# Two projections moved to the other pool of PSUM banks, a gate projection in two passes, and the last statistics drawn together

## The chip, the cores and the metric

The kernel runs on one core of one Trainium2 chip. The metric is the device time of one execution in microseconds. Three runs of the kernel before gave 1345.57, 1344.99 and 1338.48 us (median 1344.99). The profiled execution took 1340.82 us, of which 1338.9 us are the span from its first to its last instruction.

## The reference

The program is a two-layer decoder trunk on 512 positions of 1024 channels, in float32. Each layer normalises, makes one wide projection, runs four token mixers on slices of it, projects back, and adds a gated feed-forward block:

```python
for l in range(DEPTH):                      # DEPTH = 2
    h = rms_norm(x, norm_mix_w[l])
    proj = h @ w_in[l]                      # 1024 -> 3592 columns
    rq, rk, rv, rg, ca, cg, gq, gk, gv, gg, gb, ga, hq, hf, hi, hgate = split(proj)
    ret  = head_group_norm(retention(rq, rk, rv)) * silu(rg)
    conf = conformer_conv(ca, cg, ...)
    gq, gk, gv = split(silu(causal_depthwise_conv(concat(gq, gk, gv))))     # 4 taps
    gdn  = head_rms_norm(gated_deltanet(gq, gk, gv, beta=gb, a=ga)) * silu(gg)
    hg   = head_rms_norm(hgrn2(hq, hf, hi)) * silu(hgate)
    x = x + concat(ret, conf, gdn, hg) @ w_out[l]
    h = rms_norm(x, norm_ffn_w[l])
    x = x + (silu(h @ gate[l]) * (h @ up[l])) @ down[l]                     # 2816 hidden
return rms_norm(x, final_norm_w)
```

What matters here is the start of each layer: the projections `gk`, `gq` of the delta rule, each followed by a causal convolution of 4 taps and a SiLU, and its gate projection `gg` (256 gate columns with `gb` and `ga`, 264 in all). At the very end it is the last `rms_norm`.

## The kernel before, in words

Activations lie with channels on the 128 partitions and the 512 positions along the row, as eight tiles `x0` to `x7`. Every float32 product is made from three fast ones: an operand is split into a rounded high part and the rest (`xh`/`xl`, `whi`/`wlo`), and high*high, low*high and high*low are summed in one PSUM bank (`mm3`, L455 to L457). Weights come by DMA on the SP queue; ScalarE rounds them (L257), GpSimd takes the rest (L258).

PSUM has eight banks, in two pools of four. `pd` serves the projections, `pm` the mixers and the statistics. A pool hands its banks out in turn, and a matmul into a bank waits until whatever used it last is finished.

`layer` walks through `ORDER`: gk0, gk1, gq0, gq1, gg, gv0, and so on. A projection of 128 channels (`dense_c`) takes one bank: 8 blocks of input, 3 matmuls each. In layer 0 the first two go together (`dense_c2`). `gg` has positions on the partitions (`dense_t`, L493 to L495): four blocks of positions, one `pd` bank each, 96 matmuls of 264 columns.

The norm is applied after the projection. `rstd_sum` (L231) sums the squares over the channels on TensorE, VectorE scales (L235), GpSimd takes the power (L213) and writes `rst`; `rstd_spread` (L242) turns it into a row on all partitions, and ScalarE copies it into `rsb` (L246). `R_SUM` says after which projection the sum is issued; the spread follows one projection later.

What frees a bank of gk or gq is `conv4`: VectorE multiplies by `rsb` in place (L596), ScalarE makes the first tap (L598), VectorE the other three (L600), ScalarE a tanh back into the bank (L602), and VectorE the last product (L603). The two tiles `y` are shared: gk0 and gq0 use one, gk1 and gq1 the other. What frees a bank of `gg` is a tanh on ScalarE (L613), a product on VectorE (L614), and two small ones (L650, L651).

The order on each engine is not that of the code: a scheduler arranges the instructions engine by engine when the kernel is built, by its own estimate of times. On the chip each engine then goes strictly through its list.

At the end of layer 1 the last two of eight output tiles are made in two halves of 256 positions. The first half's squares are summed when all its tiles are there. `leave(half)` spreads the result, copies it to `rsb`, multiplies the eight tiles (five on VectorE from the bank, L1671, three on GpSimd from `rsb`, L1669) and issues eight DMAs of 128 KB (L1672), four each on the ScalarE and the SP queue.

Of the kernel before, what the change touches and what calls it, by code (L numbers as in the profile page):

```python
# [7 lines left out]
F32 = mybir.dt.float32  # L8
# [8 lines left out]
P = 128  # L17
T = 512
NB = T // P
D = 1024  # L20
KD = D // P
H = 4
HD = 64
G = 256
D_FF = 2816
KF = D_FF // P
DEPTH = 2
# [2 lines left out]
WARM = 4  # L30
EU, ET = 0, 0
N_OUT = 4
R_SUM = [1, 0]
TAIL = 2
CONF_POOL = 7
CHUNK_K = 2
# [30 lines left out]
           gg=2304, hq=2568, hf=2824, hi=3080, hgate=3336)  # L67
# [71 lines left out]
def kernel(  # L139
# [15 lines left out]
    V, S, GP, PE = nc.vector, nc.scalar, nc.gpsimd, nc.tensor  # L155
# [37 lines left out]
    def sm(n, name, dt=F32):  # L193
        return small.tile([P, n], dt, name=name)
# [219 lines left out]
    def w_next(keep=0):  # L414

        i = pos[2]
        pos[2] += 1
        for q in held.values():
            q[:] = [n for n in q if n >= i - keep]
        p = piece_of(items[i])  # L420
        w_split(i + 1)
        assert i in halves
        w_load(p + 3)
        w_split(i + 2)
        while pos[1] < min(i + 1 + AHEAD, len(items)) and len(items[pos[1]]) == 2 and extra:
# [17 lines left out]
    def tick():  # L443
        for it in list(active):
            if it[3] > 0:
                it[3] -= 1
            elif resume(it[0], it[1] + (it[2],)) == "end":
                active.remove(it)
            else:
                it[2] += 1  # L450
                it[3] = lag_of(it[1], it[2])
# [4 lines left out]
        PE.matmul(ps, hi[:, w], al, start=False, stop=False, skip_group_check=shared)  # L456
        PE.matmul(ps, lo[:, w], ah, start=False, stop=last, skip_group_check=shared)  # L457

    def dense_c(ah, al, ks):

        hv = w_next()
        ps = pd.tile([P, T], F32, name="pd")
        for n in range(KD):
            mm3(ps, *hv[n // 4], n % 4, ah[ks[n]], al[ks[n]], n == 0, n == KD - 1)
            if n % CHUNK_K == CHUNK_K - 1:
                tick()
        return ps

    def dense_c2():

        hv = [w_next(q) for q in range(2)]
        ps = [pd.tile([P, T], F32, name="pd") for _ in range(2)]
        for k in range(KD):
            for q in range(2):
                mm3(ps[q], *hv[q][k // 4], k % 4, xh[k], xl[k], k == 0, k == KD - 1)
            tick()
        return ps

    def dense_t(n):

        per = 1 if n > 256 else 2
        ps = [pd.tile([P, T], F32, name="pd") for _ in range(NB // per)]
        for g in range(2):
            hv = w_next()
            for hf in range(2):
                hi, lo = hv[hf]
                for kk in range(2):
                    k = g * 4 + hf * 2 + kk
                    w = slice(kk * n, (kk + 1) * n)
                    for b in range(NB):  # L490
                        o = ps[b // per][:, (b % per) * n:(b % per) * n + n]
                        tk = slice(b * P, (b + 1) * P)
                        PE.matmul(o, xh[k][:, tk], hi[:, w], start=(k == 0 and b % per == 0), stop=False)  # L493
                        PE.matmul(o, xh[k][:, tk], lo[:, w], start=False, stop=False)  # L494
                        PE.matmul(o, xl[k][:, tk], hi[:, w], start=False,  # L495
                                  stop=(k == KD - 1 and b % per == per - 1))
                    if kk % CHUNK_K == CHUNK_K - 1:
                        tick()
        return [ps[b // per][:, (b % per) * n:(b % per) * n + n] for b in range(NB)]
# [87 lines left out]
    def layer(l, ar, ga, open_mix, gvp, gzp):  # L587
# [17 lines left out]
            if len(st["conv"]) == 6:  # L605
                ga.put(*st["cy2"])

        def gate_t(ps4, n=256):

            g = ar.get(4)  # L610
            gv = g.rearrange("p (b c) -> p b c", b=NB)
            for b in range(NB):
                S.activation(gv[:, b, :], ps4[b][:, :G], AF.Tanh, scale=rsh[:, b:b + 1])  # L613
                V.scalar_tensor_tensor(gv[:, b, :], gv[:, b, :], 1.0, ps4[b][:, :G], op0=ADD, op1=MUL)  # L614
            return g

        def val_t(ps4):
            v = ar.get(4)
            vv = v.rearrange("p (b c) -> p b c", b=NB)
            for b in range(NB):  # L620
                S.activation(vv[:, b, :], ps4[b], AF.Copy, scale=rst[:, b:b + 1])
            return v

# [18 lines left out]
            return f  # L642

        def ev_gg(ps4):
            st["gg"] = gate_t(ps4)
            bt = sm(NB * H, "bt")
            z = sm(NB * H, "z")
            st["bt"], st["z"] = bt, z
            for b in range(NB):
                S.activation(bt[:, b * H:(b + 1) * H], ps4[b][:, G:G + H], AF.Tanh, scale=rsh[:, b:b + 1])  # L650
                V.scalar_tensor_tensor(z[:, b * H:(b + 1) * H], ps4[b][:, G + H:G + 2 * H], rst[:, b:b + 1],  # L651
                                       vc[:, o + V_DT:o + V_DT + H], op0=MUL, op1=ADD)
# [63 lines left out]
        for ct in range(2):  # L716
# [1 line left out]
            ev[f"hf{ct}"], ev[f"hq{ct}"] = ev_hf(ct), ev_hq(ct)  # L718
            ev[f"ca{ct}"], ev[f"cg{ct}"] = ev_ca(ct), ev_cg(ct)
            ev[f"rk{ct}"], ev[f"rq{ct}"] = ev_rot("rk", ct), ev_rot("rq", ct)  # L720
        ev["gg"] = ev_gg
        for nm in ("hi", "rv"):
            ev[nm] = (lambda nm: lambda ps4: st.__setitem__(nm, val_t(ps4)))(nm)
        for nm in ("hgate", "rg"):
# [704 lines left out]
        pend = []  # L1429
        for n, nm in enumerate(ORDER):  # L1430
            if nm == "gg":
                ps = dense_t(G + 2 * H)
            elif nm in T_GROUPS:
                ps = dense_t(G)
            elif l == 0 and n < 2:
                if n == 0:
                    first = dense_c2()
                ps = first[n]
            else:
                ps = dense_c(xh, xl, range(KD))  # L1440
            pend.append((nm, ps))
            if n == R_SUM[l]:
                rstd_sum(range(NB), ssq)
            if n < R_SUM[l] + 1:
                continue
            if n == R_SUM[l] + 1:
                rstd_spread()
            for nm, ps in pend:
                while not ar.can(*NEED.get(nm[:2], ())):
                    tick()  # L1450
                ev[nm](ps)
                if nm in after:
# [12 lines left out]
    for l in range(DEPTH):  # L1465
# [47 lines left out]
        with tc.tile_pool(name=f"ffp{l}", bufs=1, reuse_waits="tile") as ffp, \  # L1513
# [149 lines left out]
            def leave(half):  # L1663

                c = slice(half * T // 2, (half + 1) * T // 2)
                pb = rstd_spread(range(2 * half, 2 * half + 2), False)
                for k in range(KD):
                    if k % 3 == 1:
                        GP.tensor_tensor(x[k][:, c], x[k][:, c], rsb[:, c], op=MUL)  # L1669
                    else:  # L1670
                        V.tensor_tensor(x[k][:, c], x[k][:, c], pb[:, c], op=MUL)  # L1671
                    (nc.sync if k % 2 else nc.scalar).dma_start(out[k * P:(k + 1) * P, c], x[k][:, c])  # L1672

            def down_plain(rows):
                order = plain_order(l, rows)
                js = (head, rest)[rows]
                for n_m, (m, c) in enumerate(order):
                    ps = pd.tile([P, T], F32, name="pd")[:, c]
                    for r in runs(rows, n_m == 0):
                        hv = w_next()  # L1680
                        for n, k in enumerate(r):
                            ph, pl = hid[k]
                            mm3(ps, *hv[n // 4], n % 4, ph[:, c], pl[:, c], k == js[0], k == js[-1])
                        finish()
                    if rows and l + 1 == DEPTH and n_m == KD:
                        rstd_sum(range(NB // 2), ssq)
                    if rows and l + 1 == DEPTH and n_m == KD + 1:
                        leave(0)
                    V.tensor_tensor(x[m][:, c], x[m][:, c], ps, op=ADD)
                    if not rows:  # L1690
                        continue
                    if l + 1 < DEPTH:
                        split_x(m, o + NV + V_NMIX)
                        ssq_add(m)
                        nc.sync.dma_start(xs[m * P:(m + 1) * P, :], x[m])
                    else:
                        end = n_m == len(order) - 1
                        sq = ssq_add(m, end, c)
                        S.activation(x[m][:, c], x[m][:, c], AF.Copy, scale=col(V_FIN + m))
                return sq if rows and l + 1 == DEPTH else None  # L1700
# [99 lines left out]
```

## Time and profile before

| | us |
|---|---|
| three runs | 1345.57, 1344.99, 1338.48 |
| profiled execution | 1340.82 |
| its span | 1338.9 |
| TensorE busy | 1289.4 (96%) |
| VectorE busy | 897.7 (67%) |
| GpSimd busy | 799.3 (60%) |
| ScalarE busy | 707.7 (53%) |

A row of the timeline has the start, the time until the group's end, the engine, the line and operation, the tiles written and read, the size and the count; in brackets stands how long the engine was idle before it, and who ended that. PE is TensorE, DVE VectorE, ACT ScalarE, POOL GpSimd; a name with q is an engine's queue of DMA triggers. A row of a table by windows has the stretch, its length, each engine's busy time and count, then the TensorE clock that was granted (1.00 is full), the share of the DMA engines and GB/s.

### The profile page before, as it was taken

To read this page: it belongs to the slowest core of one execution; us is meant where nothing else is said; L and a number is where in the kernel's file an instruction comes from. 1 tells how busy PE (TensorE), PEld (TensorE's weight loads), DVE (VectorE), ACT (ScalarE), POOL (GpSimd) and SP (SyncE) were. 2 spreads that over 40 slices of the span, in tenths; PEclk is the share of its full clock that TensorE was granted. 3 is DMA by queue.
4 is the path that set the end of the run, shared out by engine and by line. 5 is a ranking of instruction groups with operands and counts; after the bars stand their busy time and mean duration, and the time that the engine had idled before them with its cause. 6 is when DMAs were issued, how large, how long until landed. Compare 5 with 4: busy or idle time off the path is not lost.

```text
span 1338.9 us, 23722 instructions
## 1 busy us (share of the span) xinstructions
PE 1289.4 (96%) x8984; PEld 1178.5 (88%) x8984; DVE 897.7 (67%) x1569; ACT 707.7 (53%) x1454; POOL 799.3 (60%) x669
## 2 busy tenths in 40 slices
PE   8799998899999999999999999989999999999996
PEld 6788888887889999999878889889888999999995
DVE  6743678656696866776466348786559777678645
ACT  5452553534456656665445445445445665566554
POOL 6276773764356676577454767747624666566762
PEclk9899998889999999999999999989999999999998
DMA  7223210134142333333442332102423243333322
GB/s 283 64 63 105 82 32 9 33 102 134 33 126 95 111 114 95 108 110 89 127 165 81 88 95 59 32 1 63 153 77 102 80 121 101 111 97 109 119 80 71
DMA packets 60385, 124.50 MB, mean 93 GB/s; under 512 B 17520, under 2 KB 26992, under 8 KB 60272
## 3 DMA queue, kind: packets, MB, share of 16 engines
q1 hardware_dynamic: 58832, 121.83, 29.8%
q8 instruction: 70, 1.15, 0.3%
q10 hardware_dynamic: 1440, 1.18, 0.3%
q14 instruction: 43, 0.35, 0.1%
HBM read 116.17 MB, written 6.82 MB: 92 GB/s over the span
## 4 chain that ended last, share of the span: by engine, by line
PE 84%; DVE 8%; POOL 3%; ACT 3%; issue 1%; DMA 0%; POOLq 0%; SPq 0%; ACTq 0%; DVEq 0%
PE pm L455 12%; PE pm L456 12%; PE pm L457 12%; PE pd L455 11%; PE pd L456 11%; PE pd L457 10%; PE pd L493 3%; PE pd L494 3%; PE pd L495 3%; PE pm L1167 2%; DVE x L1270 2%; PE pm L906 1%; POOL wlo L258 1%; PE pm L1040 1%; PE pm L1029 1%
## 5 line engine op out<-in xcount | busy, mean ns | idle before, releaser
L258 POOL TENSOR_TENSOR wlo<-wraw,whi 128x512 fp32r<-128x512 f32 (+2 forms) x192 | 260.6, 1366 | 226.0 <-ACT whi L257 197.2
L384 POOL TENSOR_TENSOR wlo<-wraw,whi 128x512 fp32r<-128x512 f32 x208 | 272.4, 1329 | 104.9 <-ACT whi L383 100.1
L455 PE MATMUL pm<-bh,whi 128*128 128x256 f32 x1008 | 282.7, 282 | 3.7 <-ACT pm L1623 2.0
L456 PE MATMUL pm<-bl,whi 128*128 128x256 f32 x1008 | 281.4, 280 | 0.0
L457 PE MATMUL pm<-bh,wlo 128*128 128x256 f32 x1008 | 276.8, 280 | 0.0
L257 ACT CAST whi<-wraw 128x512 fp32r<-128x512 f32 (+2 forms) x212 | 125.2, 598 | 195.8 <-PE pd L456 123.3
L455 PEld LDWEIGHTS pm<-bh,whi 128*128 128x128 f32 x1008 | 189.6, 188 | 6.7 <-DVE pm L1633 2.9
L456 PEld LDWEIGHTS pm<-bl,whi 128*128 128x128 f32 x1008 | 190.0, 188 | 0.5
L457 PEld LDWEIGHTS pm<-bh,wlo 128*128 128x128 f32 x1008 | 187.7, 188 | 0.1
L456 PE MATMUL pd<-xl,whi 128*128 128x512 f32 x416 | 165.5, 400 | 2.4 <-DVE xl L252 2.3
L455 PE MATMUL pd<-xh,whi 128*128 128x512 f32 x416 | 164.9, 399 | 0.7 <-ACT xh L251 0.4
L457 PE MATMUL pd<-xh,wlo 128*128 128x512 f32 x416 | 165.0, 399 | 0.0
L383 ACT CAST whi<-wraw 128x512 fp32r<-128x512 f32 x208 | 126.7, 624 | 50.5 <-PE pm L456 41.5
L384 DVE TENSOR_TENSOR wlo<-pd,whi 128x512 fp32r<-128x512 f32 x156 | 107.5, 689 | 52.1 <-ACT whi L383 49.6
L383 ACT CAST whi<-pd 128x512 fp32r<-128x512 f32 x156 | 92.0, 589 | 64.2 <-PE pm L456 22.7
L378 POOL TENSOR_TENSOR wraw<-wraw 128x512 f32<-128x512 f32 x52 | 68.7, 1322 | 79.0 <-DVE pd L366 66.4
L493 PE MATMUL pd<-whi,xh 128*128 128x256 f32 (+1 forms) x320 | 95.9, 301 | 15.0 <-DVE ar L603 8.5
L456 PEld LDWEIGHTS pd<-xl,whi 128*128 128x128 f32 x416 | 79.0, 190 | 21.4 <-DVE xl L252 4.3
L455 PEld LDWEIGHTS pd<-xh,whi 128*128 128x128 f32 x416 | 79.0, 190 | 19.9 <-ACT xh L251 1.8
L494 PE MATMUL pd<-wlo,xh 128*128 128x256 f32 (+1 forms) x320 | 95.4, 299 | 0.0
L495 PE MATMUL pd<-whi,xl 128*128 128x256 f32 (+1 forms) x320 | 95.1, 298 | 0.0
L457 PEld LDWEIGHTS pd<-xh,wlo 128*128 128x128 f32 x416 | 78.7, 189 | 17.4
(354 smaller groups left out, 3117.7 us busy)
## 6 DMA issues: line engine op xcount, KB each, us to landing
wraw<-in_wf_dram SPq DMA_DIRECT2D x88, 512.0 KB, 3.6
wraw<-in_wc_dram SPq DMA_DIRECT2D x34, 512.0 KB, 3.6
wraw<-in_wd_dram SPq DMA_DIRECT2D x32, 512.0 KB, 3.8
wraw<-in_wt_dram SPq DMA_DIRECT2D x16, 512.0 KB, 3.6
wraw<-in_wo_dram SPq DMA_DIRECT2D x32, 256.0 KB, 2.6
x<-in_xt_dram SPq DMA_DIRECT2D x16, 256.0 KB, 3.6
wraw<-in_wd_dram SPq DMA_DIRECT2D x16, 256.0 KB, 2.7
wraw<-in_wd_dram SPq DMA_DIRECT2D x20, 128.0 KB, 2.1
```

The source lines that it names most:

```text
L257: S.copy(hi[:, :n], r)
L258: eng.tensor_tensor(lo[:, :n], r, hi[:, :n].bitcast(F32), op=SUB)
L378: GP.tensor_tensor(src, c, a, op=SUB)
L383: S.copy(hi, src)
L384: eng.tensor_tensor(lo, src, hi.bitcast(F32), op=SUB)
L455: PE.matmul(ps, hi[:, w], ah, start=first, stop=False, skip_group_check=shared)
L456: PE.matmul(ps, hi[:, w], al, start=False, stop=False, skip_group_check=shared)
L457: PE.matmul(ps, lo[:, w], ah, start=False, stop=last, skip_group_check=shared)
L493: PE.matmul(o, xh[k][:, tk], hi[:, w], start=(k == 0 and b % per == 0), stop=False)
L494: PE.matmul(o, xh[k][:, tk], lo[:, w], start=False, stop=False)
L495: PE.matmul(o, xl[k][:, tk], hi[:, w], start=False, stop=(k == KD - 1 and b % per == per - 1))
L1167: PE.matmul(ps[:, (bb * 2 + ct) * P:(bb * 2 + ct + 1) * P], k[:, ct * T + b * P:ct * T + (b + 1) * P], qx[:, (ct * NB + b) * P:(ct * NB + ...
```

## The change

Four edits. The first two projections of each layer take `pm` banks in place of `pd` banks. In layer 0 the sum of squares is issued one projection earlier (`R_SUM`). `gg` is computed in two passes of two blocks of positions, each with two `pd` banks, and each pass is evacuated by itself; the split weights of both input halves stay until the second pass has used them. And at the end `leave(0)` comes behind the second half's sum of squares.

```diff
-R_SUM = [1, 0]
+R_SUM = [0, 0]
...
+    def w_ahead():
+        for q in held.values():
+            q[:] = [n for n in q if n >= pos[2] - 1]
+        w_split(pos[2] + 1)
...
-    def dense_c(ah, al, ks):
+    def dense_c(ah, al, ks, ps=None):
         hv = w_next()
-        ps = pd.tile([P, T], F32, name="pd")
+        if ps is None:
+            ps = pd.tile([P, T], F32, name="pd")
...
     def dense_c2():
         hv = [w_next(q) for q in range(2)]
-        ps = [pd.tile([P, T], F32, name="pd") for _ in range(2)]
+        ps = [pm.tile([P, T], F32, name="pm") for _ in range(2)]
...
+    def dense_t_wide(n):
+        hv = []
+        for part in range(2):
+            blocks = range(2 * part, 2 * part + 2)
+            ps = {b: (pd.tile([P, T], F32, name="pd")[:, :n], True, True) for b in blocks}
+            for g in range(2):
+                if part == 0:
+                    hv.append(w_next(g))
+                elif g:
+                    w_ahead()
+                t_part(ps, hv[g], n, g, blocks)
+            yield {b: ps[b][0] for b in blocks}
...
             if nm == "gg":
-                ps = dense_t(G + 2 * H)
+                while not ar.can(*NEED[nm]):
+                    tick()
+                for ps in dense_t_wide(G + 2 * H):
+                    ev_gg(ps)
+                continue
...
-                ps = dense_c(xh, xl, range(KD))
+                ps = dense_c(xh, xl, range(KD), pm.tile([P, T], F32, name="pm") if n < 2 else None)
...
-                    if rows and l + 1 == DEPTH and n_m == KD + 1:
-                        leave(0)
...
                 rstd_sum(range(NB // 2, NB), ssq, sq)
+                leave(0)
                 leave(1)
```

`t_part` holds the three matmuls and the loops that `dense_t` had. Line numbers of the changed kernel are higher by 6 to 27: L486 to L488 there are L493 to L495 before, L619 is L596, L621 is L598, L623 is L600, L625 is L602, L626 is L603, L636 is L613, L637 is L614, L673 is L650, L674 is L651, L1698 is L1671.

TensorE, layer 0, around `gg`. Tile numbers tell the banks: before, `pd_427` takes the bank that gk0 (`pd_262`) had.

```order
L455 MATMUL pd_395<-xh6_90,whi_326 128x512
L242 MATMUL pm_355<-cs_73,rst_102 128x128 x4
L456 MATMUL pd_395<-xl6_98,whi_326 128x512
...
L493 MATMUL pd_427<-whi_387,xh0_84 128x264
L494 MATMUL pd_427<-wlo_388,xh0_84 128x264
L495 MATMUL pd_427<-whi_387,xl0_92 128x264
```

In the changed kernel, `pd_395` is still gq1, `pd_427` and `pd_428` are two free banks (gk0 and gk1 lie in `pm`), and `pd_508` takes the bank of gq0 (`pd_353`), `pd_509` that of gq1:

```order
L461 MATMUL pd_395<-xh6_90,whi_349 128x512
L242 MATMUL pm_320<-cs_73,rst_102 128x128 x4
L462 MATMUL pd_395<-xl6_98,whi_349 128x512
...
L486 MATMUL pd_427<-whi_387,xh0_84 128x264
...
L486 MATMUL pd_428<-whi_435,xh7_91 128x264
L487 MATMUL pd_428<-wlo_436,xh7_91 128x264
L488 MATMUL pd_428<-whi_435,xl7_99 128x264
L486 MATMUL pd_508<-whi_387,xh0_84 128x264
L487 MATMUL pd_508<-wlo_388,xh0_84 128x264
L488 MATMUL pd_508<-whi_387,xl0_92 128x264
```

The spread (L242) stands behind the same matmul of gq1 in both; all of the first pass stands ahead of the second.

VectorE, the same stretch of layer 0, before. `pd_262`/`pd_263` are gk0/gk1, `pd_330`/`pd_395` gq0/gq1, `ar2_2`/`ar2_1` the two shared tiles `y`.

```order
L600 SCALAR_TENSOR_TENSOR ar2_2_251<-pd_262,vc_74,ar2_2_251 128x511
L600 SCALAR_TENSOR_TENSOR ar2_1_250<-pd_263,vc_74,ar2_1_250 128x511
L603 SCALAR_TENSOR_TENSOR ar4_1_362<-pd_262,ar2_2_251 128x4x128
L603 SCALAR_TENSOR_TENSOR ar4_2_370<-pd_263,ar2_1_250 128x4x128
L600 SCALAR_TENSOR_TENSOR ar2_2_251<-pd_330,vc_74,ar2_2_251 128x509
...
L603 SCALAR_TENSOR_TENSOR ar4_2_370<-pd_395,ar2_1_250 128x4x128
L614 SCALAR_TENSOR_TENSOR ar4_1_547<-ar4_1_547,pd_427 128x256
```

And in the changed kernel (`pm_262`/`pm_263` are gk0/gk1, `pd_353`/`pd_395` gq0/gq1):

```order
L623 SCALAR_TENSOR_TENSOR ar2_2_251<-pm_262,vc_74,ar2_2_251 128x511
L623 SCALAR_TENSOR_TENSOR ar2_1_250<-pm_263,vc_74,ar2_1_250 128x511
L637 SCALAR_TENSOR_TENSOR ar4_1_499<-ar4_1_499,pd_427 128x256
L637 SCALAR_TENSOR_TENSOR ar4_1_499<-ar4_1_499,pd_428 128x256
L626 SCALAR_TENSOR_TENSOR ar4_1_327<-pm_262,ar2_2_251 128x4x128
L626 SCALAR_TENSOR_TENSOR ar4_2_335<-pm_263,ar2_1_250 128x4x128
L674 SCALAR_TENSOR_TENSOR z_498<-pd_427,rst_102,vc_74 128x4
L674 SCALAR_TENSOR_TENSOR z_498<-pd_428,rst_102,vc_74 128x4
L623 SCALAR_TENSOR_TENSOR ar2_2_251<-pd_353,vc_74,ar2_2_251 128x509
```

The first pass's evacuation (two L637, two L674) now stands between gk's convolution and gq's. ScalarE's list has its part at the same place: the two tanh of the gate (L636) ahead of gk's two (L625), and the two small ones (L673) ahead of gq's first taps (L621). In layer 1 the first pass's L637 stand later, behind gq's taps and only ahead of gq's two last products (L626).

TensorE, the end of the program, before (`pm_14984` is the first half's sum, `pm_15032` the second's):

```order
L231 MATMUL pm_14984<-cs_73,ssq_100 128x1 x2
L242 MATMUL pm_15008<-cs_73,rst_102 128x128 x2
L231 MATMUL pm_15032<-cs_73,ssq_100 128x1 x2
L231 MATMUL pm_15032<-cs_73,sq_15029 128x1 x2
L242 MATMUL pm_15040<-cs_73,rst_102 128x128 x2
```

and in the changed kernel:

```order
L231 MATMUL pm_14984<-cs_73,ssq_100 128x1 x2
L231 MATMUL pm_15012<-cs_73,ssq_100 128x1 x2
L231 MATMUL pm_15012<-cs_73,sq_15009 128x1 x2
L242 MATMUL pm_15020<-cs_73,rst_102 128x128 x2
L242 MATMUL pm_15040<-cs_73,rst_102 128x128 x2
```

The first half's spread moved behind the second half's sums. On GpSimd the second power (L213) moved ahead of the first half's three products, on VectorE the second scaling (L235) ahead of its five. ScalarE's list is as before: copy to `rsb`, four DMA triggers, copy to `rsb`, four DMA triggers.

More of the change, by code (lines that the diff above doesn't have):

```diff
@@ L467, in dense_c, with t_part @@
         return ps
+    def t_part(ps, hv, n, g, blocks):
+        for hf in range(2):
+            hi, lo = hv[hf]
+            for kk in range(2):
+                k = g * 4 + hf * 2 + kk
+                w = slice(kk * n, (kk + 1) * n)
+                for b in blocks:
+                    o, first, last = ps[b]
+                    tk = slice(b * P, (b + 1) * P)
+                    PE.matmul(o, xh[k][:, tk], hi[:, w], start=(k == 0 and first), stop=False)
+                    PE.matmul(o, xh[k][:, tk], lo[:, w], start=False, stop=False)
+                    PE.matmul(o, xl[k][:, tk], hi[:, w], start=False, stop=(k == KD - 1 and last))
+                if kk % CHUNK_K == CHUNK_K - 1 and (len(blocks) == NB or hf):
+                    tick()
     def dense_c2():
         hv = [w_next(q) for q in range(2)]
-        ps = [pd.tile([P, T], F32, name="pd") for _ in range(2)]
+        ps = [pm.tile([P, T], F32, name="pm") for _ in range(2)]
         for k in range(KD):
@@ L479, in dense_t @@
     def dense_t(n):
-        per = 1 if n > 256 else 2
-        ps = [pd.tile([P, T], F32, name="pd") for _ in range(NB // per)]
+        banks = [pd.tile([P, T], F32, name="pd") for _ in range(NB // 2)]
+        ps = {b: (banks[b // 2][:, (b % 2) * n:(b % 2) * n + n], b % 2 == 0, b % 2 == 1) for b in range(NB)}
         for g in range(2):
[L484 to L499, printed above, removed]
+            t_part(ps, w_next(), n, g, range(NB))
+        return {b: ps[b][0] for b in range(NB)}
+    def dense_t_wide(n):
[10 more added lines that the diff above has]
+            yield {b: ps[b][0] for b in blocks}
     dram = ctx.enter_context(tc.tile_pool(name="dram", bufs=1, space=bass.MemoryType.DRAM))
@@ L606, in conv4, with gate_t @@
                 ga.put(*st["cy2"])
-        def gate_t(ps4, n=256):
-            g = ar.get(4)
+        def gate_t(ps4, g=None):
+            g = g or ar.get(4)
             gv = g.rearrange("p (b c) -> p b c", b=NB)
-            for b in range(NB):
+            for b in ps4:
                 S.activation(gv[:, b, :], ps4[b][:, :G], AF.Tanh, scale=rsh[:, b:b + 1])
@@ L619, in val_t @@
             vv = v.rearrange("p (b c) -> p b c", b=NB)
-            for b in range(NB):
+            for b in ps4:
                 S.activation(vv[:, b, :], ps4[b], AF.Copy, scale=rst[:, b:b + 1])
@@ L644, in ev_gg @@
         def ev_gg(ps4):
[L645 to L649, printed above, removed]
+            if "bt" not in st:
+                st["bt"], st["z"], st["gg"] = sm(NB * H, "bt"), sm(NB * H, "z"), ar.get(4)
+            bt, z = st["bt"], st["z"]
+            gate_t(ps4, st["gg"])
+            for b in ps4:
                 S.activation(bt[:, b * H:(b + 1) * H], ps4[b][:, G:G + H], AF.Tanh, scale=rsh[:, b:b + 1])
@@ L1431, in layer @@
             if nm == "gg":
-                ps = dense_t(G + 2 * H)
+                while not ar.can(*NEED[nm]):
+                    tick()
+                for ps in dense_t_wide(G + 2 * H):
+                    ev_gg(ps)
+                continue
             elif nm in T_GROUPS:
```

1 line of the change is left out of this document (removed).

## The prediction

> **What bounds the kernel now.** I read the page's head first, then TensorE's waits, then the timeline at the three places that the change touches.
>
> ```profile
> span 1338.9 us, 23722 instructions
> PE 1289.4 (96%) x8984; PEld 1178.5 (88%) x8984; DVE 897.7 (67%) x1569; ACT 707.7 (53%) x1454; POOL 799.3 (60%) x669
> ...
> PE pd L493 <- DVE ar L603: 8.5, 2, 6.7
> PE pm L1040 <- DVE ar L1035: 3.1, 2, 1.9
> ```
>
> TensorE is busy for 1289.4 of 1338.9 us, and the change removes none of its matmuls. So it can win only idle TensorE time (49.6 us in all) and matmuls at a reduced clock. The longest wait is the one that the change addresses: the gate projection `gg` (L493) waits 8.5 us in two layers for the last product of a convolution (L603), 6.7 of it in layer 0. In the timeline:
>
> ```profile
> 32.46 1.05 PE L242 MATMUL pm<-cs,rst 128*128 128x128 f32 x8
> 34.05 0.39 PE L456 MATMUL pd<-xl,whi 128*128 128x512 f32 x1
> 34.28 0.40 PE L457 MATMUL pd<-xh,wlo 128*128 128x512 f32 x1
> 41.41 0.59 PE L493 MATMUL pd<-whi,xh 128*128 128x264 f32 x1 [6.73 <-DVE ar L603]
> 47.07 0.29 PE L494 MATMUL pd<-wlo,xh 128*128 128x264 f32 x1
> 55.73 0.39 PE L455 MATMUL pd<-xh,whi 128*128 128x512 f32 x1
> ...
> 700.83 0.40 PE L457 MATMUL pd<-xh,wlo 128*128 128x512 f32 x1
> 702.98 0.39 PE L493 MATMUL pd<-whi,xh 128*128 128x264 f32 x1 [1.75 <-DVE ar L603]
> 714.79 0.39 PE L455 MATMUL pd<-xh,whi 128*128 128x512 f32 x1
> ...
> 42.00:45.00 3.00, 3.00 (x15) 3.00 (x15) 2.90 (x6) 0.73 (x2) 0.00 (x0) 0.50 0.00 0
> 48.00:51.00 3.00, 3.00 (x27) 3.00 (x26) 0.78 (x3) 1.10 (x3) 0.00 (x0) 1.00 0.00 0
> 705.00:710.00 5.00, 5.00 (x43) 5.00 (x42) 4.77 (x9) 2.29 (x5) 0.00 (x0) 1.00 0.22 90
> ```
>
> The reader is to see two prices. Layer 1's 96 matmuls of `gg` run from 702.98 to 714.79, 11.8 us at clock 1.00, so a pass of 48 costs 5.9. Layer 0's take 41.41 to 55.73, 14.3 us: after the 6.73 us wait the granted clock is 0.50 until about 47.07, which costs 14.3 - 11.8 = 2.5 us more. The wait in layer 1 is only 1.75 us, and the clock stays full.
>
> **Layer 0, step by step.** The earlier sum of squares (`R_SUM`) gives nothing: the power is long done when the spread (the row at 32.46) comes up in TensorE's list, and in the changed list the spread stands behind the same matmul of gq1.
>
> ```profile
> 26.33 1.02 POOL L213 TENSOR_TENSOR rst<-ms,mhalf 128x4 f32<-128x4 f32 x1
> 27.32 2.79 POOL L258 TENSOR_TENSOR wlo<-wraw,whi 128x528 fp32r<-128x528 f32 x2
> ...
> 36.57 4.02 DVE L600 SCALAR_TENSOR_TENSOR ar<-pd,vc,ar 128x509 f32<-128x509 f32 x6
> 40.66 1.35 DVE L603 SCALAR_TENSOR_TENSOR ar<-pd,ar 128x512 f32<-128x512 f32 x2
> 42.11 4.03 DVE L600 SCALAR_TENSOR_TENSOR ar<-pd,vc,ar 128x509 f32<-128x509 f32 x6
> 46.22 1.35 DVE L603 SCALAR_TENSOR_TENSOR ar<-pd,ar 128x512 f32<-128x512 f32 x2
> 50.22 0.79 DVE L614 SCALAR_TENSOR_TENSOR ar<-ar,pd 128x256 f32<-128x256 f32 x2 [2.66 <-ACT ar L613]
> 50.98 0.59 DVE L651 SCALAR_TENSOR_TENSOR z<-pd,rst,vc 128x4 f32<-128x4 f32 x2
> ...
> 40.03 1.26 ACT L602 ACTIVATE pd<-ar 128x512 f32<-128x512 f32 x2 [3.71 <-DVE ar L600]
> 41.39 1.34 ACT L598 ACTIVATE ar<-pd,vc 128x512 f32<-128x512 f32 x2
> 49.72 0.84 ACT L613 ACTIVATE ar<-pd,rsh 128x256 f32<-128x256 f32 x2 [2.88 <-PE pd L495]
> 50.68 0.63 ACT L650 ACTIVATE bt<-pd,rsh 128x4 f32<-128x4 f32 x2
> ```
>
> All weights of `gg` are split by 30.1 (the row at 27.32), so the first pass starts on its two free banks when gq1 ends, at 34.28 + 0.23 = 34.5, and ends at 34.5 + 5.9 = 40.4: the old wait is filled. The second pass needs the banks of gq0 and gq1, which are free only after gq's convolution, and that is now later. With the durations above: gk's taps end at 40.6 as before. ScalarE first does the gate's two tanh (L613's 0.84, ready with the pass's end: 40.2 to 41.05), then gk's (1.26, to 42.3). VectorE does the gate's two products (0.79, to 41.5), then gk's two (first at 41.75 behind its tanh, to 43.1), then `z` (0.59, to 43.65). ScalarE meanwhile does L650's pair (0.63, to 42.95) and gq's first taps. So gq's six taps start at 43.65 in place of 42.11, and end at 47.7; with the same distance from there to the last products (46.22 - 42.11 = 4.1), gq0's bank is free at about 48.4 in place of 46.9, and gq1's at 49.1. The work put ahead of them costs 1.5 us.
>
> The second pass starts at 48.4, an idle time of 8.0 us behind the first. It is longer than the 6.73 that brought the clock to 0.50, so I let it pay the same 2.5: the end is 48.4 + 5.9 + 2.5 = 56.8, against 55.73. Layer 0 **loses 1.1 us**. The bounds are no cold matmuls (54.3, a gain of 1.4) and a pass that is cold throughout (48.4 + 2 * 5.9 = 60.2, a loss of 4.5); the value is the one nearest to a measured wait of this length.
>
> [...]
>
> **Layer 1.** Here the projections are followed by less waiting, and the first pass's evacuation stands behind gq's taps.
>
> ```profile
> 703.68 4.03 DVE L600 SCALAR_TENSOR_TENSOR ar<-pd,vc,ar 128x509 f32<-128x509 f32 x6 [0.16 <-ACT ar L598]
> 707.79 1.35 DVE L603 SCALAR_TENSOR_TENSOR ar<-pd,ar 128x512 f32<-128x512 f32 x2
> ```
>
> The first pass runs from 701.1 to 707.0. gq's taps end at 707.7 as before, then the gate's two products (0.79) come ahead of gq's last ones: gq0's bank is free at 707.75 + 0.79 + 0.67 = 709.2. TensorE idles 2.2 us in place of 1.75 and ends at 709.2 + 5.9 = 715.1, against 714.79: **a loss of 0.3 us**. If 2.2 us are enough to lower the clock, 2.5 us come on top.
>
> The projections behind `gg` wait for the same evacuations as before, so they move with its end.
>
> **The end.** The first half's statistics were ahead of the second's on three engines, and the second's waited behind the first half's products:
>
> ```profile
> 1326.56 0.42 ACT L221 ACTIVATE sq<-x 128x256 f32<-128x256 f32 x1 [0.46 <-DVE x L1689]
> 1327.42 0.71 PE L242 MATMUL pm<-cs,rst 128*128 128x128 f32 x4 [1.02 <-POOL rst L213]
> 1328.17 0.37 ACT L246 COPY rsb<-pm 128x256 f32<-128x256 f32 x1 [0.66 <-PE pm L242]
> 1328.58 1.75 DVE L1671 TENSOR_TENSOR x<-x,pm 128x256 f32<-128x256 f32 x5 [1.98 <-ACT rsb L246]
> 1329.03 1.87 ACTq L1672 DMA_DIRECT2D out_dram<-x  x4
> 1332.68 0.37 ACT L246 COPY rsb<-pm 128x256 f32<-128x256 f32 x1 [4.14 <-PE pm L242]
> 1333.09 1.75 DVE L1671 TENSOR_TENSOR x<-x,pm 128x256 f32<-128x256 f32 x5 [2.69 <-ACT rsb L246]
> ...
> DMA  0000000002999999999900003999999999900000
> ```
>
> Now the second half's spread is ready by 1329.2, but its copy to `rsb`, on which the products of both engines wait, stands on ScalarE behind the first half's four triggers (1329.03 + 1.87 = 1330.9). The first half's spread waits for the square at 1326.56 (ends 1326.98) and four short matmuls, 0.15 us later than before. So the copy starts at 1330.9 + 0.15 = 1331.05 in place of 1332.68: 1.6 us by the chain of operations. The last row (40 slices of 0.3 us from 1327 on) shows another limit: each half's DMAs fill the engines for 3.1 us, 1329.9 to 1333.0 and 1334.4 to 1337.5, with a gap of 1.4. The gap is all there is to win, less the 0.15: **a gain of 1.2 us**, between 0.8 (if some of the gap stays between the halves) and 1.4.
>
> **Between these places.** The scheduler also shifts some rows of the mixers. The largest: in layer 0 a state product of the delta rule (L1077) comes behind 22 matmuls of a projection.
>
> ```profile
> 173.68 0.71 PE L1077 MATMUL pm<-ar,ar 128*128 128x128 f32 x4 [0.98 <-ACT ar L1070]
> ...
> 210.00:215.00 5.00, 5.00 (x38) 4.50 (x38) 3.69 (x6) 3.16 (x7) 2.30 (x2) 0.59 0.11 39
> ```
>
> That hides the 0.98 us and delays the chain by 22 * 0.23 = 5.1 us (0.23 is the pitch of those matmuls, 34.05 to 34.28); a block later the lists agree again, and the wait has to be paid there. Gain bound: the two waits quoted (L1040's 3.1 and this 0.98), about 4. Loss bound: 5.1 - 1.0 = 4.1. Nothing speaks for one side, so 0.
>
> **Sum.** +1.1 + 0.3 - 1.2 + 0 = +0.2 us on the profiled 1340.82, so 1341.0. That execution lies between the runs shown; the four together average 1342.5, and I predict 1342.7 for a run: **no change that can be measured**. The terms' bounds together reach from -1.4 - 1.4 - 4 = -6.8 to 4.5 + 2.8 + 4.1 - 0.8 = +10.6, ends that would need every term to fall on one side.
>
> **Rivals.** (a) The wait simply goes: the first pass covers it, gq's convolution isn't delayed, the clock never falls. Then 6.73 + 2.5 + 1.75 are won and 1.2 at the end, 1342.5 - 12.2 = 1330.3. For it speaks that TensorE's wait names gk's product alone; against it that gq's bank was free only at 46.9 even before, 6.5 us behind the first pass's end. (b) The wait in layer 1, grown to 2.2 us, lowers the clock: 1342.7 + 2.5 = 1345.2. For it speaks the row 210:215, clock 0.59, shortly behind a wait of 1.9 us (L1040); there the matmuls around it are small ones, here they are dense, which is against it. (c) Slower: the delta rule's chain of layer 0 doesn't recover its 5.1 us, and its back part, which TensorE waits for in the stretch around 205 to 225, comes 4.1 us later on balance; as the clock there is already 0.59, a further 5 us slice at that rate adds 2.1, and the time is 1342.7 + 4.1 + 2.1 = 1348.9. It decides if the levels of the second pair (L1040) start over 1 us later than now. Against it: VectorE's list has the second pair's base ahead of the delayed state copies, so that its input comes no later. That the two passes aren't there isn't a rival: the list shows them.
>
> **How the numbers follow.** The forecast has 0.72, (a) 0.09, (b) 0.13, (c) 0.06. About 0.5% (6.7 us) is what a measurement of this kernel can tell from no change; its own three runs lie 7 us apart. Faster by more is (a) and 0.02 of the scatter, 0.11; (c) ends about at that bound, so half of it and as much of the scatter make slower 0.05; the rest, 0.84, is no change. The range goes from 1336.5 to 1348: the forecast with the scatter of the runs, and (b).
>
> **What would show it.** In the changed profile: the first pass starts within 0.3 us of gq1's end; a second wait of 7 to 9 us ahead of `pd_508`'s first matmul, released by L626, with the clock at 0.50 behind it; `gg` ends near 56.8 and, in layer 1, 715.1; DMAs of the end without a gap. I would be wrong if the second wait is under 4 us, if the clock stays full behind it, or if a mixer's stretch moves by more than 3 us.

## The result and the profile after

The change made the kernel faster: 1332.09 us median (1330.16 to 1336.27, 12 runs) against 1340.65 us (1332.05 to 1345.57, 12 runs), a ratio of 0.9948 with a 95% interval of 0.9931 to 0.9964. The prediction, 1342.7 us and no change that can be measured, was wrong, and the time lies below its range. In two later sessions the same instructions stood at 0.9954 (0.9933 to 0.9974; built without the edit to `R_SUM`, which turns out to change nothing) and 0.9959 (0.9937 to 0.9981).

The head of the page of the changed kernel, and its view of TensorE's waits (total, times, longest):

```profile
span 1331.6 us, 23717 instructions
PE 1287.8 (97%) x8984; PEld 1177.3 (88%) x8984; DVE 897.5 (67%) x1569; ACT 705.5 (53%) x1454; POOL 788.4 (59%) x669
```

```profile
PE pm L1062 <- DVE ar L1057: 5.3, 5, 2.0
PE pd L486 <- DVE x L1292: 3.4, 1, 3.4
PE pd L486 <- DVE z L674: 2.6, 1, 2.6
...
PE pd L486 <- DVE ar L626: 2.0, 1, 2.0
```

The row that headed this view before (8.5 us in two waits, 6.7 the longest) is gone. In its place stand 2.6 us in layer 0, released by `z` (L674), which is the evacuation of `gg` itself, and 2.0 us in layer 1, released by a convolution's last product (L626). TensorE's timeline at both places, start and length in us:

```profile
36.24 0.39 PE L463 MATMUL pd<-xh,wlo 128*128 128x512 f32 x1
36.47 0.28 PE L486 MATMUL pd<-whi,xh 128*128 128x264 f32 x1
...
42.18 0.28 PE L488 MATMUL pd<-whi,xl 128*128 128x264 f32 x1
45.07 0.56 PE L486 MATMUL pd<-whi,xh 128*128 128x264 f32 x1 [2.60 <-DVE z L674]
...
48.48 0.28 PE L486 MATMUL pd<-whi,xh 128*128 128x264 f32 x1
...
52.50 0.39 PE L461 MATMUL pd<-xh,whi 128*128 128x512 f32 x1
...
693.75 0.29 PE L486 MATMUL pd<-whi,xh 128*128 128x264 f32 x1
...
701.72 0.39 PE L486 MATMUL pd<-whi,xh 128*128 128x264 f32 x1 [1.97 <-DVE ar L626]
...
707.70 0.39 PE L461 MATMUL pd<-xh,whi 128*128 128x512 f32 x1
```

The stretch behind the wait in layer 0 (start:end and length, busy time of PE, PEld, DVE, ACT and POOL, then TensorE's granted clock) is at half clock:

```profile
45.07:48.50 3.43, 3.43 (x16) 3.43 (x17) 3.43 (x6) 0.45 (x1) 0.00 (x0) 0.51 0.00 0
```

Layer 0: the first pass begins the moment gq1 ends (36.47), runs 6.0 us, waits 2.6, and the second pass ends at 52.50. From gq1's end that is 16.0 us, where it was 55.73 - 34.51 = 21.2: **5.2 us are won**. In three further profiles whose layer 0 is as before (experiments 1 and 4, and layer 1's banks alone in experiment 3) that stretch took 20.4 to 21.0, with fewer matmuls at half clock (with layer 1's banks alone for 5.2 us behind the wait, before for 5.66), so the gain is 4.4 to 5.2, 4.8 on average. Layer 1: from the first pass's start to the end 13.95 us (693.75 to 707.70). Before, `gg` began 1.92 us later, counted from the spread (L242), and ran 11.8 us, 13.7 in all: 0.2 us are lost. What the second pass of layer 0 waits for is to be seen in the timelines of VectorE and ScalarE:

```profile
42.65 0.78 DVE L637 SCALAR_TENSOR_TENSOR ar<-ar,pd 128x256 f32<-128x256 f32 x2
43.51 1.29 DVE L626 SCALAR_TENSOR_TENSOR ar<-pm,ar 128x512 f32<-128x512 f32 x2
44.71 0.34 DVE L674 SCALAR_TENSOR_TENSOR z<-pd,rst,vc 128x4 f32<-128x4 f32 x2
44.97 4.02 DVE L623 SCALAR_TENSOR_TENSOR ar<-pd,vc,ar 128x509 f32<-128x509 f32 x6
49.37 1.29 DVE L626 SCALAR_TENSOR_TENSOR ar<-pd,ar 128x512 f32<-128x512 f32 x2 [0.38 <-ACT pd L625]
...
42.14 0.84 ACT L636 ACTIVATE ar<-pd,rsh 128x256 f32<-128x256 f32 x2 [3.86 <-PE pd L488]
42.88 1.12 ACT L625 ACTIVATE pm<-ar 128x512 f32<-128x512 f32 x2
```

The second pass starts at 45.07, right behind the second `z` (44.71 + 0.34). gq's convolution is then still at its taps (44.97 to 49.0), and its last products come at 49.37. So in layer 0 the second pass does not use gq's banks at all. It uses those of the first pass.

The banks that the tiles received in the built programs, by number (0 to 3 are `pd`, 4 to 7 `pm`):

| | gk0, gk1 | gq0, gq1 | gg, first two blocks | gg, last two blocks |
|---|---|---|---|---|
| before, layer 0 | 0, 3 | 2, 1 | 0, 3 | 2, 1 |
| changed, layer 0 | 4, 7 | 0, 3 | 2, 1 | **2, 1** |
| changed, layer 1 | `pm` | 0, 1 | 3, 2 | 0, 1 |

The sentences ahead of the prediction that "a pool hands its banks out in turn", and that `pd_508` takes the bank of gq0, are therefore wrong for layer 0: the banks received are those that come free first in the scheduler's order, since `z` stands ahead of gq's taps in VectorE's list.

The end of the program: the two copies to `rsb` in ScalarE's timeline, and the DMA engines' busy share in 40 slices from 1319 us on:

```profile
1321.26 0.37 ACT L246 COPY rsb<-pm 128x256 f32<-128x256 f32 x1 [0.71 <-PE pm L242]
...
1324.03 0.37 ACT L246 COPY rsb<-pm 128x256 f32<-128x256 f32 x1 [2.40 <-POOL x L1696]
```

```profile
DMA  0000000000002999999999978965999996000000
```

The second copy follows 2.8 us behind the first (before 4.5), and the gap in the DMA row has shrunk to a dent. From the first half's sum of squares to the end it is 12.66 us, against 13.0 before. That is less than forecast, but it is one execution; more of them below.

### The profile page after: what moved, and what is told of

It is laid out like the page before. It is cut to its first block, busy times and chain, and to the rows that moved or that the text cites. A ratio compares the mean times of both kernels' runs of the same rounds, so it can differ in the third digit from the quotient of the medians.

```text
span 1331.6 us, 23717 instructions
## 1 busy us (share of the span) xinstructions
PE 1287.8 (97%) x8984; PEld 1177.3 (88%) x8984; DVE 897.5 (67%) x1569; ACT 705.5 (53%) x1454; POOL 788.4 (59%) x669
## 3 DMA queue, kind: packets, MB, share of 16 engines
q8 instruction: 71, 1.16, 0.4%
## 4 chain that ended last, share of the span: by engine, by line
PE 82%; DVE 8%; POOL 5%; ACT 3%; issue 2%; DMA 0%; SPq 0%; POOLq 0%; ACTq 0%; DVEq 0%
PE pm L461 12%; PE pm L462 12%; PE pm L463 12%; PE pd L461 10%; PE pd L462 10%; PE pd L463 10%; PE pd L486 2%; PE pm L1189 2%; PE pd L488 2%; PE pd L487 2%; POOL wlo L258 2%; DVE x L1292 1%; PE pm L928 1%; ACT whi L383 1%; PE pm L1062 1%
## 5 line engine op out<-in xcount | busy, mean ns | idle before, releaser
L258 POOL TENSOR_TENSOR wlo<-wraw,whi 128x512 fp32r<-128x512 f32 (+2 forms) x192 | 248.9, 1305 | 227.3 <-ACT whi L257 186.7
L461 PE MATMUL pd<-xh,whi 128*128 128x512 f32 x384 | 151.6, 396 | 0.6 <-DVE x L729 0.6
L463 PE MATMUL pd<-xh,wlo 128*128 128x512 f32 x384 | 151.9, 396 | 0.0
L462 PE MATMUL pd<-xl,whi 128*128 128x512 f32 x384 | 151.6, 396 | 0.0
L486 PE MATMUL pd<-whi,xh 128*128 128x256 f32 (+1 forms) x320 | 94.2, 295 | 8.0 <-DVE x L1292 3.4
L488 PE MATMUL pd<-whi,xl 128*128 128x256 f32 (+1 forms) x320 | 93.5, 293 | 0.0
L461 PEld LDWEIGHTS pd<-xh,whi 128*128 128x128 f32 x384 | 72.3, 188 | 16.7 <-DVE x L729 0.8
L462 PEld LDWEIGHTS pd<-xl,whi 128*128 128x128 f32 x384 | 72.2, 188 | 16.0
L463 PEld LDWEIGHTS pd<-xh,wlo 128*128 128x128 f32 x384 | 72.2, 188 | 15.9
```

The lines of the kernel that those rows point to most:

```text
L258: eng.tensor_tensor(lo[:, :n], r, hi[:, :n].bitcast(F32), op=SUB)
L461: PE.matmul(ps, hi[:, w], ah, start=first, stop=False, skip_group_check=shared)
L486: PE.matmul(o, xh[k][:, tk], hi[:, w], start=(k == 0 and first), stop=False)
L488: PE.matmul(o, xl[k][:, tk], hi[:, w], start=False, stop=(k == KD - 1 and last))
```

## The experiments

All times are medians, and the kernel before ran beside each group (its medians there: 1341.35, 1337.99 and 1340.18 us).

**1. Two passes alone.** gk0 and gk1 back in `pd`, sum of squares and end as before:

```diff
-        ps = [pm.tile([P, T], F32, name="pm") for _ in range(2)]
+        ps = [pd.tile([P, T], F32, name="pd") for _ in range(2)]
...
-                ps = dense_c(xh, xl, range(KD), pm.tile([P, T], F32, name="pm") if n < 2 else None)
+                ps = dense_c(xh, xl, range(KD))
```

> The kernel before with only the gate projection in two passes (gk0 and gk1 stay in pd, sum of squares and end as before). My theory now: this edit alone moves nothing, because the scheduler had already issued gg's matmuls as 48 into two banks and then 48 into two others. Time within 0.3% of the kernel before, the wait of 6.7 us ahead of gg unchanged, and any difference between the two profiles is the clock of single stretches. Rival: evacuating each pass by itself lets the second one start earlier; then layer 0's gg ends 1 to 5 us earlier and the time is 1336 to 1340 against 1340.7.

1339.53 us (12 runs), ratio 0.9982 (0.9963 to 1.0001). Once scheduled, this program is the kernel before, instruction for instruction, with the same banks and waits. The kernel before was written as one pass of four blocks, but the scheduler had issued it as 48 matmuls into two banks and then 48 into two others. Of the four edits, this one by itself does nothing. Its profile is thus a second one of the kernel before. First TensorE's wait around `gg` in layer 0, then two stretches of the mixers (columns as above):

```profile
PE pd L486 <- DVE ar L626: 6.7, 1, 6.7
```

```profile
77.61:82.52 4.91, 4.91 (x39) 4.55 (x38) 3.15 (x8) 2.90 (x6) 2.60 (x3) 1.00 0.37 107
269.63:293.01 23.38, 22.16 (x141) 18.96 (x140) 11.81 (x25) 9.49 (x17) 14.13 (x17) 1.00 0.38 124
```

The same two stretches of the same instructions, in the profile of before:

```profile
78.19:84.67 6.48, 6.48 (x38) 5.75 (x37) 4.72 (x11) 2.89 (x6) 2.60 (x3) 0.74 0.27 83
274.23:300.69 26.46, 25.25 (x142) 21.60 (x141) 11.79 (x25) 9.49 (x17) 14.08 (x17) 0.87 0.39 110
```

1.6 and 3.1 us of difference without any difference in the program: the clock stayed full in one execution (1.00 in both rows) and fell in the other (0.74 and 0.87). The two spans are 1330.9 and 1338.9 us. Two profiles therefore can't be subtracted as a whole. Only stretches at the same clock can.

**2. The banks alone.** The kernel before with gk0 and gk1 in `pm`, `gg` written in one pass of four blocks:

```diff
-        ps = [pd.tile([P, T], F32, name="pd") for _ in range(2)]
+        ps = [pm.tile([P, T], F32, name="pm") for _ in range(2)]
...
-                ps = dense_c(xh, xl, range(KD))
+                ps = dense_c(xh, xl, range(KD), pm.tile([P, T], F32, name="pm") if n < 2 else None)
```

> The kernel before with only gk0 and gk1 in pm banks (gg written in one pass of four blocks, end as before). My theory: this is the whole gain of the projections. Layer 0 from gq1's end to gg's end takes about 16 us in place of 21.2, the second pass waits 2.6 us for the first one's own evacuation; time 1332 to 1334. Rival: the two passes are needed as well, since one pass of four blocks must wait for gq's banks; then the wait stays at 7 us or more and the time is 1339 to 1345.

1333.71 us (8 runs), 0.9951 (0.9929 to 0.9972). TensorE's waits between 30 and 60 us:

```profile
PE pd L494 <- DVE z L652: 2.6, 1, 2.6
```

The same wait, released by the same `z`: the scheduler again put the last two blocks into the first two's banks. Up to the last statistics this program is the changed kernel, instruction for instruction. The banks of gk0 and gk1 are the whole effect on the projections.

**3. Layer 0's banks alone** (the first line of the diff above), **and layer 1's alone** (the second).

> Only layer 0's gk0 and gk1 in pm banks, everything else as before. My theory: layer 0 gives the 5 us and layer 1 nothing, so 1333 to 1336, and layer 1's gg waits 1.7 us for a convolution's last product as before. Rival: layer 1 carries part of the gain (its mixers' order differs); then this one stays 2 us or more behind gk_pm.

> Only layer 1's gk0 and gk1 in pm banks, everything else as before. Theory: layer 1's gg begins 1.9 us earlier and ends 0.2 us later, counted from the spread, with a wait of 2.0 us for gq's convolution between its passes: the time is that of the kernel before within 1 us. Rival: layer 1 gives 1 us or more through the mixers' order.

Layer 0 alone: 1334.78 us (12 runs), 0.9953 (0.9932 to 0.9974), as much as both. Layer 1 alone: 1337.20 us (12 runs), 0.9973 (0.9948 to 0.9999). Its `gg`, from the spread on to the end of its last matmul, took 7.39 + 14.09 = 21.5 us against 21.3 before, so that stretch wins nothing, as expected; but the time was 3 us lower, which I had not expected and which fits the rival. The mean granted clock of these runs was 0.9808 against 0.9779, and experiment 8 asks what that is worth.

**4. The end alone.**

```diff
-                    if rows and l + 1 == DEPTH and n_m == KD + 1:
-                        leave(0)
...
                 rstd_sum(range(NB // 2, NB), ssq, sq)
+                leave(0)
                 leave(1)
```

> The kernel before with only the first half's output behind the second half's statistics. My theory: the second half's products start 1.7 us earlier, but then the 2.1 MB of the output keep the DMA engines full; from the last residual sum's start to the end 12.5 us in place of 12.8, time 0.3 us below before. Rival (the prediction's term): the gap of 1.4 us between the halves' transfers goes, less 0.15: 1.2 us below before.

1339.62 us (12 runs), 0.9988 (0.9967 to 1.0009): too little for the time to tell. The DMA row of its end, in slices of 0.3 us from 1325 us on:

```profile
DMA  0000000000000005999999999999999999950000
```

No gap, and 11.61 us from the sum of squares to the end. My expectation (12.5, a gain of 0.3) came from the changed kernel's first profile and fell; the prediction's term holds. Over all profiles of this study the stretch took 12.57 to 13.54 us in the five without this edit (mean 13.0) and 11.55 to 12.71 in the eight with it (mean 11.9): a gain of 1.1 us.

**5. The state that the prediction worked out.** The second pass is written into gq0's and gq1's own tiles, and gv0 and gv1 behind it, so that they can't be moved ahead:

```diff
-            ps = {b: (pd.tile([P, T], F32, name="pd")[:, :n], True, True) for b in blocks}
+            ps = {b: (own[b - 2] if part else pd.tile([P, T], F32, name="pd"))[:, :n] for b in blocks}
+            ps = {b: (ps[b], True, True) for b in blocks}
...
+            if nm in ("gq0", "gq1"):
+                own.append(ps)
```

> The changed kernel with gg's second pass written into the very banks of gq0 and gq1 (and gv0, gv1 into the same two afterwards, so that they can't be moved ahead of it). This is the state that the prediction worked out. Theory: the prediction failed at the choice of the bank alone. Then the second pass starts about 13.5 us behind gq1's end (prediction: 13.9), after an idle time of 7 to 8 us, released by the convolution's last product, its first 5 to 6 us run at half clock, and gg ends 5.5 to 6.5 us later than in the changed kernel, counted from gq1's end; with gv0's wait for gg's evacuation the time is 1339 to 1342. Rival: the working itself was off (the convolution isn't delayed, the clock isn't lowered): gg's end moves by less than 3 us and the time stays under 1336.

1345.09 us (12 runs), 1.0049 (1.0026 to 1.0073): slower than before. TensorE's timeline in layer 0, and the stretch behind the wait (its clock is the number behind POOL's busy time):

```profile
34.77 0.39 PE L463 MATMUL pd<-xh,wlo 128*128 128x512 f32 x1
35.00 0.28 PE L486 MATMUL pd<-whi,xh 128*128 128x264 f32 x1
...
48.65 0.59 PE L486 MATMUL pd<-whi,xh 128*128 128x264 f32 x1 [7.65 <-DVE ar L627]
...
53.42 0.28 PE L486 MATMUL pd<-whi,xh 128*128 128x264 f32 x1
...
56.71 0.40 PE L461 MATMUL pd<-xh,whi 128*128 128x512 f32 x1
```

```profile
48.65:53.42 4.77, 4.77 (x21) 4.77 (x22) 0.54 (x1) 0.00 (x0) 0.00 (x0) 0.50 0.00 0
```

An idle time of 7.65 us (prediction 8.0), released by the convolution's last product, 4.77 us at half clock behind it, and `gg`'s end 21.7 us behind gq1's (prediction 56.8 - 34.5 = 22.3). With gq's banks the prediction's working of layer 0 comes true within 0.6 us, and the time lies in its range. The time itself is 3 us above my expectation. `gg` ends 5.7 us later than in the changed kernel, and the stretches from there to the delta rule's first small matmuls are 1.5 and 1.6 us longer in the two layers, of which 1.0 and 0.9 are a wait of the projection behind `gg` for `z`. Together that is 8.8 us; at the same clock (experiment 8) the program is 10.5 us slower than the changed kernel, and I did not follow the rest up.

**6. No wait at all.** The second pass in the two free `pm` banks, run twice:

```diff
-            ps = {b: (pd.tile([P, T], F32, name="pd")[:, :n], True, True) for b in blocks}
+            pool, nm = ((pd, "pd"), (pm, "pm"))[part]
+            ps = {b: (pool.tile([P, T], F32, name=nm)[:, :n], True, True) for b in blocks}
```

> The changed kernel with the second pass of gg in the two pm banks that are free, so that it waits for no evacuation. Theory (in each layer the second pass' wait is what is left of the stall): layer 0 gets rid of 2.6 us and of the half clock behind it (1.5 us), layer 1 of 2.0 us; 1332.1 - 6 = 1326. Rival: what follows takes it back, because the gates, on which the delta rule's chain waits, are evacuated behind the convolution as before; then 1330 to 1333.

> The second pass in pm banks once more, beside the changed kernel in the same session. Theory: the 6.5 us that gg loses in the two layers come out of the time less about 2 us that the mixers behind it take back: 3 to 5 us below the changed kernel. Rival: the earlier difference was the clock's scatter; then within 1.5 us of it.

1329.59 us (7 runs), 0.9922 (0.9893 to 0.9951), and 1329.74 us (12 runs), 0.9929 (0.9906 to 0.9951), beside 1334.61 us for the changed kernel in the same session. This version beats both kernels, by some 4 to 5 us over the changed one.

Layer 0 in the profile of the first of them: the second pass's first matmul in the timeline, and three stretches (`gg`, the projections up to the delta rule's first small matmuls, and the stretch behind):

```profile
40.78 0.29 PE L486 MATMUL pm<-whi,xh 128*128 128x264 f32 x1
```

```profile
34.95:46.80 11.85, 11.85 (x98) 11.85 (x97) 11.27 (x21) 7.11 (x15) 4.34 (x4) 1.00 0.14 47
46.80:70.26 23.46, 23.46 (x103) 19.00 (x103) 17.98 (x39) 15.11 (x33) 13.23 (x12) 1.00 0.36 112
70.26:77.24 6.98, 6.98 (x41) 6.32 (x39) 5.22 (x15) 2.80 (x6) 1.96 (x3) 0.76 0.26 77
```

The last two stretches in the changed kernel:

```profile
52.66:74.96 22.30, 22.30 (x97) 18.07 (x97) 15.15 (x35) 12.93 (x30) 13.12 (x12) 1.00 0.39 112
74.96:79.86 4.90, 4.90 (x39) 4.55 (x38) 3.14 (x8) 2.90 (x6) 2.82 (x4) 1.00 0.36 135
```

`gg` takes 11.85 us in one piece at full clock, in layer 1 11.83. That wins 4.3 + 2.3 us in the two layers, and not all of it arrives. The second stretch is 1.16 us longer, but that is no loss: five further matmuls of the projections stand in it, at 0.23 us each, and come out of what follows. The third holds two further ones; the rest of its 2.08 us, about 1.6, is lost to the clock, which falls there in both profiles of this kernel (0.76 and 0.75); in the changed kernel's first profile and in that of its repetition it is 1.00 (74.96:79.86 and 73.64:78.55). TensorE has no wait there for the gates, so the rival's reason does not show as a wait. So 1326 was not reached; the programs' means lie 3.9 us apart, and about 1 us more is not traced.

**7. Smaller questions.** `bt` and `z` ahead of the gate's products in the evacuation, the earlier sum of squares undone, and the changed kernel once more:

```diff
             bt, z = st["bt"], st["z"]
-            gate_t(ps4, st["gg"])
             for b in ps4:
...
+            gate_t(ps4, st["gg"])
...
-R_SUM = [0, 0]
+R_SUM = [1, 0]
```

> The changed kernel with the two small products (bt, z) ahead of the gate's products in gg's evacuation. Theory: in layer 0 the second pass' bank is released by the gate's product in place of z, 0.3 us earlier or later (both stand behind the two last products of gk's convolution in VectorE's list): same time within 1 us of 1332.1. Rival: the smaller wait keeps the clock up, and 1.5 us are won in layer 0.

> The changed kernel with R_SUM = [1, 0] as before. Theory: nothing is issued otherwise, so it is a repetition of the changed kernel: 1332 within 2 us, and its profile differs from the changed kernel's by the clock of single stretches and by the transfers of the end alone. Rival: the earlier sum of squares carries part of the gain; then 1 us or more slower, with the spread (L242) later against gq1's matmuls.

> The changed kernel once more: 1331.5 to 1334, and the transfers of the end take about 1 us less than in its first profile (11.6 us from the sum of squares to the end in place of 12.66), if that was scatter. Rival: the end gains only 0.3 us in this kernel, 12.6 us again.

1332.88, 1333.98 and 1334.61 us (12, 10 and 12 runs; 0.9946, 0.9954 and 0.9959, each about 0.002 wide to both sides). With `z` first the wait in layer 0 is 2.5 us and ends with the gate's product:

```profile
PE pd L486 <- DVE ar L637: 2.5, 1, 2.5
```

Both orders stand behind gk's last products on VectorE, so little changes, as expected: the stretch to `gg`'s end is 0.3 us shorter in layer 0, and layer 1's wait is 1.6 us in place of 2.0. The mean is 1.4 us lower (experiment 8), more than these two give. The repetition of the changed kernel lies 0.6 us above what I had expected. The kernel without the earlier sum of squares is, once scheduled, the changed kernel with every instruction, bank and wait: that edit does nothing either. In its second profile the changed kernel's end took 11.55 us and, without the edit to `R_SUM`, 11.57, so the 12.66 of its first profile was scatter.

**8. The same clock.** Every run lists its span and its mean granted clock, and the spans follow the clock: the program before goes from 1342.2 us on average at 0.974 (11 runs) to 1331.2 at 0.983 (9 runs). A straight line through each program's runs, one slope for all, falls by 1.1 us for each 0.001 of clock. At 0.978 it gives (with intervals of about 95%):

| program | runs | mean time, us | mean clock | span at clock 0.978, us |
|---|---|---|---|---|
| before (with two passes alone) | 102 | 1339.8 | 0.9779 | 1337.9 ± 0.3 |
| changed (with both repetitions) | 34 | 1333.6 | 0.9790 | 1332.6 ± 0.5 |
| banks, both layers | 8 | 1334.3 | 0.9789 | 1333.2 ± 0.9 |
| banks, layer 0 | 12 | 1335.1 | 0.9781 | 1333.1 ± 0.8 |
| banks, layer 1 | 12 | 1336.8 | 0.9808 | 1337.7 ± 0.8 |
| end alone | 12 | 1339.2 | 0.9778 | 1337.1 ± 0.8 |
| second pass in `pm` | 19 | 1329.7 | 0.9801 | 1329.9 ± 0.6 |
| second pass in gq's banks | 12 | 1345.6 | 0.9775 | 1343.1 ± 0.8 |
| `z` first | 12 | 1332.2 | 0.9789 | 1331.2 ± 0.8 |

At the same clock layer 0's banks are worth 4.8 us, layer 1's 0.1, the end 0.8; the sum, 5.7, is the changed kernel's 5.3 within the errors, which leaves nothing for the mixers that they could show. The rest of the 6.2 us between the means, about 1, goes with the changed kernel's slightly higher clock. The half clock around `gg` itself counts in that mean: in the profiles it was granted for 3.4 us in the changed kernel (45.00 to 48.42) and for 10.2 before (36.83 to 47.07), and 3.4 us at 0.50 are already 0.0013 of the mean clock over a span of 1331.6 us. So that 1 us may be the change's own, and the table may understate layer 0 a little. Whether layer 1's order of instructions raises the clock, or its 12 runs were lucky, stays open; the kernels with both layers' banks (0.9789 and 0.9790) do not show such a clock.

## Why the prediction was right or wrong

**The step that failed** is "The second pass needs the banks of gq0 and gq1", in layer 0. It rested on the assumption that a pool hands out its banks strictly in turn. The second pass took the first one's banks, so it waited 2.6 us in place of 8.0, for the first pass's evacuation in place of a convolution. That is the prediction's own sign of being wrong, a second wait under 4 us. Experiment 5 forces the assumed banks and gets the predicted wait (7.65), clock (0.50) and end (21.7 us behind gq1, 22.3 predicted); experiment 2 shows that the scheduler picks the others by itself. The evidence was at hand: VectorE's list in the part on the change has `z` of the first pass ahead of gq's taps, so the first pass's banks come free about 5 us before gq's (45.05 and 50.0).

Point by point:

- **The first pass fills the old wait**: right. It starts at gq1's end and takes 6.0 us (5.9 predicted).
- **Its evacuation delays gq's convolution by 1.5 us**: too much. gq's taps start 44.97 - 36.47 = 8.5 us behind gq1's end, before 42.11 - 34.51 = 7.6, so 0.9. It no longer mattered to the second pass.
- **The clock behind the wait, 2.5 us**: right in kind, too large for the shorter wait. It was one execution's, too: behind the same 6.73 us `gg` lost 1.7 us in experiment 1 (41.61 to 55.15, less 11.8). The second pass took 52.50 - 45.07 = 7.4 us, 1.5 more than 5.9. Layer 0 in all: 6.0 + 2.6 + 7.4 = 16.0 us, predicted 22.3, before 21.2. The term was +1.1 and is -5.2, or -4.8 against all four profiles of before.
- **Layer 1, +0.3**: right: a wait of 2.0 us (2.2 predicted) for gq's product, since there the second pass does get gq's banks, and +0.2 in the stretch.
- **The end, -1.2**: right. The gap closes, and it is -1.1 over the profiles, -0.8 by the table.
- **The mixers, 0**: right at the same clock. Single profiles differ there by up to 7 us for the same instructions (layer 0's mixers took 271.5 and 264.4 us in two profiles of the program before), so the criterion "if a mixer's stretch moves by more than 3 us" could not have shown anything.
- **`R_SUM`, 0**: right, and more strictly than argued. That the passes are new was wrong: the list of before has two passes already.
- **The base**: 1342.5 was the mean of four runs. The program before has a mean of 1339.8 in 102, so 2.7 us of the miss were in the starting point. From there 1339.8 - 4.8 + 0.3 - 1.2 = 1334.1, where the changed kernel's 34 runs average 1333.6. The idle time of 49.6 us in the prediction is 49.5 by its own figures, which changes nothing.

Of the rivals, (a), 1330.3 with 0.09, came nearest in time, but not for its reason: gq's convolution is in the way of nothing in layer 0 because its banks aren't used there, a wait of 2.6 us is left, and the clock does fall. (b), half clock behind layer 1's wait, happened in one profiled execution of the changed program: not in the profile above, but in that of the repetition, where the second pass's matmuls have a pitch of 0.22 us from 703.11 to 705.97 and of 0.12 behind that, and the stretch from the first pass's start took 15.56 us at a mean clock of 0.89:

```profile
694.77:710.33 15.56, 13.59 (x98) 13.38 (x97) 8.28 (x16) 7.12 (x15) 2.81 (x3) 0.89 0.13 35
```

In the changed kernel's first profile the same stretch took 14.11 us, at full clock:

```profile
693.75:707.86 14.11, 12.14 (x98) 11.92 (x97) 8.28 (x16) 7.12 (x15) 2.84 (x3) 1.00 0.13 39
```

(c) has no trace: layer 0's mixers took 263.9 to 269.7 us in the changed program's three profiles, against 264.4 and 271.5 in the two of the program before.

## What to carry to other kernels

Before you price a wait for a buffer, establish which buffer it is from the issued order of whoever reads the candidates last; here the scheduler took the one that was free first, and a loop written in another order left the schedule untouched. An idle stretch of the bound engine is best filled with banks that nobody else holds: here the pool with two banks lying free took the whole wait away, where the pool in use left 2.6 and 2.0 us. Take the base from many runs, and compare single profiles only over stretches with the same granted clock.

## What the runs showed of the hardware

- Behind a wait of 2.60 us the granted clock was 0.51 (the row 45.07:48.50 above), with matmuls at a pitch of 0.22 us in place of 0.12. Behind one of 1.97 us it fell in one execution of the changed program (0.89 over 694.77:710.33) and stayed full in another (1.00 over 693.75:707.86).
- The time at half clock behind a wait did not follow the length of the wait: 3.4 us behind 2.60, 4.77 behind 7.65, and behind the same 6.73 us 5.66 before the change (41.41 to 47.07), 5.2 with layer 1's banks alone (43.19 to 48.36) and 3.9 in experiment 1 (41.61 to 45.52). Before the change the clock fell before the wait ended: it is 0.50 from 36.83 on, 2.2 us behind gq1's last matmul and 4.6 us ahead of the first of `gg`.
- The clock also fell without any wait of TensorE in the profile: in the rows 78.19:84.67 (0.74) and 77.61:82.52 (1.00) TensorE is busy throughout (6.48 and 4.91 us), with the same short matmuls at the start. The scatter of this kernel, 1332 to 1345 us for one and the same program, goes for the most part with the mean granted clock (spans of 1342.2 us at 0.974 and 1331.2 at 0.983, experiment 8); how much of it comes from stretches without a wait is not shown.
